# Hybrid decoder layer on one core: the sums of weight blocks spread otherwise over the weight loads

## The chip, the cores and the metric

The kernel runs on one core of one Trainium2 chip. The metric is the device time of one execution in microseconds (us), smaller is better. The core has a matrix engine (TensorE, PE in the profile, its weight loads PEld), three engines for elementwise work (VectorE: DVE, ScalarE: ACT, GpSimd: POOL), and 16 DMA engines that are fed here by two queues: SP's (the profile's q1) and POOL's (q0).

## The reference

One layer over 512 positions of width 1024, all in float32:

```python
h = rms_norm(x, norm_mix)
hq, hf, hi, hg, mq, mk, mv = split(h @ w_in)          # one projection, 3584 columns
o_hgrn = hgrn2_mixer(hq, hf, hi, hg, lb, hgrn_norm)   # gated linear recurrence, chunks of 32
o_moba = moba_attention(rotary(mq), rotary(mk), mv)   # causal attention over chosen blocks
x = x + concat(o_hgrn, o_moba) @ w_out
h, mem_n = rms_norm(x, norm_xattn), rms_norm(mem, norm_mem)     # mem: 256 tokens
x = x + cross_attention(h, mem_n, w_q, w_k, w_v, w_o)           # 4 heads
h = rms_norm(x, norm_mlp)
x = x + square(relu(h @ w_ff1)) @ w_ff2               # 1024 -> 4096 -> 1024
out = rms_norm(x, norm_final)
```

## The kernel before

**Weight units.** All weights pass through the core as units of 128 rows by 1024 columns (512 KB), in the order in which PE uses them. Units 0 to 3 belong to the columns hf, 4 to 7 to hi, 8 to 11 to hq, 12 to 15 to mv, 16 to 23 to mq and mk (`mkq`), 24 to 27 to hg. From unit 28 (`W_WO`) a list named `line` sets the order: the eight units of the out-projection (`wo`) and the eight of the cross-attention query (`xq`), mixed with units of the memory products (keys and values of the 256 memory tokens; `memX`, `memY` in the profile), and last the eight units `xo` of the cross-attention's output. Unit 80 (`MLP`) begins the first MLP product in 8 groups (`j`) of 7 steps (`s`), unit 136 (`FF2`) the second MLP product.

**What happens to a unit.** SP's queue loads it from DRAM into a raw buffer `wr` (there are three, `RAWS`). Each float32 product is made as three matmuls of a high and a low part: ACT makes the high part `wh` of the weights, DVE the remainder `wl`, and with the end of that DVE instruction the raw buffer is free for a later unit. `need(u)` stands at the start of a unit's matmuls; it issues the splits up to two units ahead (`SPLIT_AHEAD`) and as many loads as there are raw buffers, which makes five units ahead. Instructions of an engine run in the order of the program. In the stretch of units 8 to 12 that order has, besides the splits, the work of the recurrence: DVE makes decayed queries `qx` and keys `ke`, and PE multiplies them (`a`, `ket`).

**The sums.** The memory products and both MLP products are computed with seven block products instead of eight. For that some weight blocks are added to others beforehand, in DRAM, by transfers alone: `copy` (L237) goes on SP's queue, `add` (L240) is an accumulating transfer on POOL's queue, and `values` (L269) are plain transfers on POOL's queue. For the memory weights the sums go to four pairs of blocks, `m0` to `m3` (`MU`), for the second MLP weight to 24 units `u0`, `u1`, `u2` (`FU`). The generator `all_sums()` gives these 88 steps in one fixed order: values into m0 (each step two transfers of 256 KB), adds into m0, four copies into m2, values into m3 (four steps of two transfers), four copies into m1, eight adds into m2 and m1, four adds into m3; then 16 copies into u0 and u2, 16 adds into u0 and u2, 8 copies into u1, 16 adds into u1. `more_sums()` issues the next step, whatever it is, and binds it to `marks[-2]`, the last matmul in front of the previous `need`: so the step's transfers wait until that matmul is done.

Where `more_sums()` is called sets the time of each sum: in `load_unit`, as often as `sums_after(u)` says, right behind the load of unit u; in `need` for the last units ahead of the MLP; and in `f1_prep`, once in a group of the first MLP product. `sums_after` gave two steps with each load of units 8 to 11 and from 16 on, three from 22 on, two with each load of `wo`, one with each of `xo`.

Of the kernel before, what the change touches and what calls it, by code (L numbers as in the profile page):

```python
# [31 lines left out]
W_HG, W_WO, W_MEMK, W_XQ, W_MEMV, W_XO, W_MLP = 24, 28, 36, 44, 52, 60, 68  # L32
MEM_P = 7
MEM_UNITS = 2 * MEM_P * 2
MLP = W_MLP - 16 + MEM_UNITS
# [90 lines left out]
def hybrid_layer(ctx: ExitStack, tc: tile.TileContext, xT, memT, ws, vecs, consts, rots, out):  # L126
# [91 lines left out]
    line, keys = [], iter(KEYS + VALUES)  # L218
# [86 lines left out]
    def more_sums():  # L305
        dma = next(transfers, None)
        for d in dma if isinstance(dma, list) else [dma] if dma is not None else ():
            tc.add_manual_dep(d.ins, marks[-2].ins.name, AFTER)
# [6 lines left out]
    def load_unit():  # L315
        u = state["load"]
        raws[u] = raw_tile(f"wr{u}", u >= FF2 and (u - FF2) % 2 == 1)
        if len(sources[u].shape) == 3:
            SY.dma_start(raws[u].rearrange("p (n c) -> p n c", n=4), sources[u])
        else:  # L320
            SY.dma_start(raws[u], sources[u])
        state["load"] += 1
        for _ in range(sums_after(u)):
            more_sums()

    def sums_after(u):

        if u < W_WO:
            return 2 * (8 <= u < 12 or u >= 16) + (u >= 22)
        if u < MLP:  # L330
            return {"wo": 2, "xo": 1}.get(line[u - W_WO][0], 0)
        return u % 2 == 0 and (4 <= u - FF2 < 14 or u - FF2 >= 26)

    W_MV = 12
# [5 lines left out]
    def split_raw(u, raw, a, b, eng=None):  # L340
        rounded = A.activation(his[u][:, a:b], raw[:, a:b], AF.Copy)
        if u == 6:
            tc.add_manual_dep(rounded.ins, first_root[0].ins.name, BEHIND)
        elif u == W_MV:
            tc.add_manual_dep(rounded.ins, last_decay[0].ins.name, BEHIND)

        def lower(hi=his[u], lo=los[u]):
            (eng or V).tensor_sub(lo[:, a:b], raw[:, a:b], hi[:, a:b].bitcast(F32))
        later(lower)
# [4 lines left out]
    def split_begin():  # L354
        u = state["split"]
        his[u] = wpool.tile([P, D], F32R, tag="whi", name=f"wh{u}", bufs=WBUFS)
        if u < MLP - 4 and u % 4 == 0:
            los[u] = ep.tile([P, D], F32R, tag="wloe", name=f"wl{u}", bufs=1)
        else:
            los[u] = wpool.tile([P, D], F32R, tag="wlo", name=f"wl{u}", bufs=WBUFS - 1)  # L360
        state["split"] += 1
        return u

    def split_unit(eng=None):
        u = split_begin()
        split_part(u, 0, D, eng)
        del raws[u]
# [7 lines left out]
    def f1_load(j, what):  # L375

        r, c = {"A": (0, 0), "B": (0, 0), "C": (1, 1), "D": (1, 0)}[what.upper()]
        t = f1raw[what, j] = raw_tile(f"w{what}{j}", what in "AD")
        nc.sync.dma_start(two(t), E[r][c][j].rearrange("n p c -> p n c"))
        if what in "Bc":  # L380
            nc.gpsimd.dma_start(two(t), E[0][1][j].rearrange("n p c -> p n c"), accum_op=ALU.add)

    def f1_add(j, out, x, y):
        V.tensor_add(f1raw[out, j], f1raw[x, j], f1raw[y, j])

    def f1_prep(j, s):

        split_raw(split_begin(), f1raw[("ABACcDd" if j == 7 else "ABADcCD")[s], j], 0, D)
        if s == 1 and j == 0:
            f1_add(j, "A", "B", "C")  # L390
        if j == 7:
            if s == 1:
                f1_load(j, "d")
                state["load"] = FF2
            elif s > 3:
                load_unit()
        elif s == 1:
            f1_load(j + 1, "B")
        elif s == 2:
            f1_load(j + 1, "A")  # L400
        elif s == 4:
            f1_load(j + 1, "c")
        elif s == 5:
            f1_load(j + 1, "C")
        elif s == 6:
            f1_load(j + 1, "D")
        if s == 2 and j < 7:
            more_sums()

    def need(u, ahead=SPLIT_AHEAD):  # L410
        marks.append(last_mm[0])
        if MLP <= u + SPLIT_AHEAD < FF2:
            f1_prep(*divmod(u + SPLIT_AHEAD - MLP, 7))
            return
        last = MLP if u < MLP else UNITS
        most = RAWS if u < MLP else 2 * RAWS
        want_load, want_split = min(last, u + LOAD_AHEAD + 1), min(last, u + ahead + 1)
        while state["split"] < want_split or state["load"] < want_load:
            if state["load"] < want_load and state["load"] - state["split"] < most:
                load_unit()  # L420
            elif state["split"] < want_split:
                split_unit()
            else:
                break
        if MLP - 6 <= u < MLP - 2:
            for what in ("A", "B", "cC", "D")[u - MLP + 6]:
                f1_load(0, what)
        if MLP - 8 <= u < MLP - 2:
            more_sums()


# [66 lines left out]
    def fm_stage(u0, act, n, evac, name, groups, order=tuple(range(KT)), o=slice(None), bank=acc_bank, between=None):  # L498


        u = 0
        at = u0 if callable(u0) else lambda n: u0 + n
        for size, late in groups:
            accs = []
            early, rest = order[:KT - late], order[KT - late:]
            for j in range(size):
                need(at(u + j))
                accs.append((bank(u + j) if between else bank)(f"{name}{u + j}"))
                for k in early:
                    fm_k(at(u + j), accs[j][:, :n], act, k, k == order[0], k == order[-1], o)  # L510
                if not late:
                    evac(u + j, accs[j])
                    if between:
                        between(u + j)
            if late:
                for j in range(size):
                    for k in rest:
                        fm_k(at(u + j), accs[j][:, :n], act, k, False, k == order[-1], o)
                    evac(u + j, accs[j])
                    if between:  # L520
                        between(u + j)
            u += size

    def tm_stage(u0, act, ntok, evac, name, beside=()):

        accs = [(side_bank if t in beside else acc_bank)(f"{name}{t}") for t in range(ntok)]
        for j in range(4):
            need(u0 + j)
            hi, lo = his[u0 + j], los[u0 + j]
            for t in range(ntok):  # L530
                for kk in range(2):
                    a_hi, a_lo = act(2 * j + kk)
                    a_hi, a_lo = a_hi[:, t * P:(t + 1) * P], a_lo[:, t * P:(t + 1) * P]
                    w_hi, w_lo = hi[:, kk * T:(kk + 1) * T], lo[:, kk * T:(kk + 1) * T]
                    st = j == 0 and kk == 0
                    mm(accs[t], a_hi, w_hi, st, False)
                    mm(accs[t], a_hi, w_lo, False, False)
                    mm(accs[t], a_lo, w_hi, False, j == 3 and kk == 1)
                if j == 3:
                    evac(t, accs[t])  # L540
# [199 lines left out]
    for k in range(KT):  # L740
        if k % 2 == 0:
            need(k // 2, SPLIT_AHEAD - (k == KT - 2))
        if k == KT - 1:
            next(norm_x)
            lower_bounds()
            ordered.__exit__(None, None, None)
        a_hi, a_lo = x_act(k)
        for hs in ((0, 1), (2, 3)) if k in (0, 2) else ((0,), (1,), (2,), (3,)):
            w = {h: [by_k(t[k // 2])[:, h, k % 2] for t in (his, los)] for h in hs}
            for h in hs:  # L750
                mm(accs[h], w[h][0], a_hi, k == 0, False)
            for h in hs:
                mm(accs[h], w[h][1], a_hi, False, False)
            for h in hs:
                mm(accs[h], w[h][0], a_lo, False, k == KT - 1)
        if k == 0:
            cols = [slice(n * P, (n + 1) * P) for n in range(QE)]
            for acc, c in zip(q_accs, cols):
                mm(acc, q_hi[:, c], a_hi, True, False)
            for acc, c in zip(q_accs, cols):  # L760
                mm(acc, q_lo[:, c], a_hi, False, False)
            for acc, c in zip(q_accs, cols):
                mm(acc, q_hi[:, c], a_lo, False, False)
# [3 lines left out]
    u = 4  # L767
# [614 lines left out]
    u = MLP  # L1382
# [437 lines left out]
```

## Time and profile before

| | us |
|---|---|
| median of three runs | 722.6 (721.71 to 723.08) |
| profiled execution | 723.61 |
| its span | 721.8 |
| PE busy | 710.6 |
| DVE busy | 578.9 |
| ACT busy | 452.4 |
| POOL busy | 81.3 |

The span is the time from the first to the last instruction of the profiled execution; the execution's own time is a little longer. PE's granted clock has a mean of 0.994 of full speed. An instruction row of the timeline reads: start, duration, engine, line, operation, output and inputs, and in brackets the idle time of the engine ahead of it and what ended it. A DMA row gives the size and the median time from issue to landing. Names are without buffer numbers, so all unit loads are called `wr<-in_ws_dram`, or `wr<-m` and `wr<-u` where a sum is loaded.

### The profile page before, as it was taken

What the parts mean: (1) busy time and instruction counts of PE and PEld (TensorE: products, weight loads), DVE (VectorE), ACT (ScalarE), POOL (GpSimd) and SP (SyncE); (2) the same over time, 40 slices, a digit from 0 to 9 for tenths busy, and PEclk for the clock granted to TensorE, in tenths of its full rate; (3) what the DMA queues carried; (4) which work ended last, traced back from release to release, by engine and by line L of the source; (5) the groups of instructions that cost most, each with busy time, mean ns of one, the idle gap of its engine ahead of it and who ended that gap; (6) DMA issues with size and microseconds to landing.
All of it is one profiled execution on the core that took longest, in us unless ns stands there. A gap on an engine that the chain in (4) does not pass through costs nothing.

```text
span 721.8 us, 10716 instructions
## 1 busy us (share of the span) xinstructions
PE 710.6 (98%) x4024; PEld 612.4 (85%) x4024; DVE 578.9 (80%) x878; ACT 452.4 (63%) x659; POOL 81.3 (11%) x98
## 2 busy tenths in 40 slices
PE   9999999999999899999999999999999999999995
PEld 7888888888888788888788989999999888888885
DVE  5899547988786677777578789989889999987886
ACT  6883585446685586666565765666558655547672
POOL 1410205100001000002201101111010100110000
PEclk9999999999999999999999999999999999999998
DMA  8795469999478855458996487778987966998523
GB/s 277 254 227 171 171 215 211 275 312 298 177 200 237 253 185 175 161 189 190 279 289 147 130 211 206 210 190 223 231 199 248 294 222 191 277 275 247 187 77 116
DMA packets 62803, 155.71 MB, mean 216 GB/s; under 512 B 5248, under 2 KB 19456, under 8 KB 62240
## 3 DMA queue, kind: packets, MB, share of 16 engines
q1 hardware_dynamic: 47552, 116.70, 46.5%
q0 software_dynamic: 14592, 37.75, 28.3%
q8 instruction: 31, 0.51, 0.3%
q10 hardware_dynamic: 608, 0.59, 0.3%
q14 instruction: 20, 0.16, 0.1%
HBM read 152.92 MB, written 48.23 MB: 279 GB/s over the span
## 4 chain that ended last, share of the span: by engine, by line
PE 95%; DMA 3%; ACT 1%; DVE 1%; issue 0%; DVEq 0%; SPq 0%; ACTq 0%
PE Y L118 16%; PE X L118 12%; PE xo L118 7%; PE XB L118 6%; PE XA L118 6%; PE mkq L118 6%; PE xq L118 6%; PE wo L118 5%; PE mv L118 3%; PE hq L118 3%; PE hf L118 3%; PE hg L118 3%; PE Z L118 3%; PE hi L118 3%; DMA wr<-in_ws_dram 2%; PE memX L118 2%
## 5 line engine op out<-in xcount | busy, mean ns | idle before, releaser
L118 DVE TENSOR_TENSOR wl<-wr,wh 128x1024 fp32r<-128x1024 f32 (+2 forms) x139 | 165.6, 1196 | 39.2 <-ACT wh L118 32.6
L118 ACT ACTIVATE wh<-wr 128x1024 fp32r<-128x1024 f32 (+2 forms) x139 | 142.7, 1036 | 79.0 <-PE X L118 16.3
L118 PE MATMUL X<-op,wh 128*128 128x512 f32 (+1 forms) x264 | 62.9, 385 | 0.0
L240 POOL DMA_DIRECT2D u<-in_ws_dram x32 | 28.1, 923 | 287.9 <-PE xt L118 90.9
L118 PEld LDWEIGHTS X<-op,wh 128*128 128x128 f32 x264 | 47.2, 189 | 8.5
L118 PE MATMUL Y<-op,wh 128*128 128x512 f32 x192 | 47.2, 391 | 0.0
L118 PEld LDWEIGHTS Y<-op,wh 128*128 128x128 f32 x192 | 35.0, 189 | 6.6
L118 PEld LDWEIGHTS X<-op,wl 128*128 128x128 f32 x256 | 33.6, 191 | 1.6
L118 PE MATMUL X<-op,wl 128*128 128x256 f32 x256 | 34.1, 282 | 0.0
L118 PE MATMUL Y<-OS,wh 128*128 128x256 f32 x256 | 33.4, 283 | 0.0
L118 PEld LDWEIGHTS Y<-OS,wh 128*128 128x128 f32 x256 | 32.5, 192 | 0.7
L118 DVE TENSOR_TENSOR op<-g,op 128x1024 fp32r<-128x1024 f32 x24 | 29.2, 1219 | 2.8 <-ACT op L118 2.8
L118 ACT ACTIVATE op<-g 128x1024 fp32r<-128x1024 f32 x28 | 29.2, 1044 | 0.4 <-PE XB L118 0.4
L118 ACT ACT_TABLE_LOAD x20 | 25.7, 1283 | 2.1 <-PEq L1808 1.2
L118 PEld LDWEIGHTS Y<-op,wl 128*128 128x128 f32 x192 | 25.3, 191 | 1.3
L118 PE MATMUL Y<-op,wl 128*128 128x256 f32 x192 | 25.7, 282 | 0.0
L118 PE MATMUL mkq<-xlo,wh 128*128 128x512 f32 x64 | 25.7, 401 | 0.0
L118 PE MATMUL xq<-x1hi,wl 128*128 128x512 f32 x64 | 25.5, 399 | 0.0
L118 PE MATMUL wo<-mixhi,wh 128*128 128x512 f32 x64 | 25.4, 396 | 0.0
L118 PE MATMUL mkq<-xhi,wl 128*128 128x512 f32 x64 | 25.4, 396 | 0.0
L118 PE MATMUL xq<-x1hi,wh 128*128 128x512 f32 x64 | 25.3, 395 | 0.0
L118 PE MATMUL mkq<-xhi,wh 128*128 128x512 f32 x64 | 25.3, 395 | 0.0
(384 smaller groups left out, 1905.9 us busy)
## 6 DMA issues: line engine op xcount, KB each, us to landing
wr<-in_ws_dram SPq DMA_DIRECT2D x87, 512.0 KB, 5.4
u<-in_ws_dram POOLq DMA_DIRECT2D x32, 512.0 KB, 8.5
wr<-u SPq DMA_DIRECT2D x32, 512.0 KB, 5.1
u<-in_ws_dram SPq DMA_DIRECT2D x16, 512.0 KB, 9.0
wr<-m SPq DMA_DIRECT2D x16, 512.0 KB, 4.1
m<-in_ws_dram POOLq DMA_DIRECT2D x12, 512.0 KB, 12.2
m<-in_ws_dram POOLq DMA_DIRECT2D x16, 256.0 KB, 5.3
u<-u SPq DMA_DIRECT2D x8, 512.0 KB, 5.7
```

The lines of the kernel that those rows point to most:

```text
L118: return f(*args, **kw)
L240: return nc.gpsimd.dma_start(dst, src, accum_op=ALU.add, max_dma_last_dim=4 * D)
```

## The change

Three tables of numbers are changed, and no computation. Two steps go with each load of units 12 to 15 too, where none did. From there on each step of the list goes with a load four units earlier, until the loads of `wo`, which get one step each instead of two. So by the last load of `wo` 54 steps have gone out in both kernels, and 62 by the last of `xo`. The extra calls in `need` begin one unit later (five instead of six), and the last group of the first MLP product makes one step as the others do.

```diff
     def sums_after(u):
         if u < W_WO:
-            return 2 * (8 <= u < 12 or u >= 16) + (u >= 22)
+            return 2 * (u >= 8) + (u >= 22)
         if u < MLP:
-            return {"wo": 2, "xo": 1}.get(line[u - W_WO][0], 0)
+            return line[u - W_WO][0] in ("wo", "xo")
...
-        if s == 2 and j < 7:
+        if s == 2:
             more_sums()
...
-        if MLP - 8 <= u < MLP - 2:
+        if MLP - 7 <= u < MLP - 2:
             more_sums()
```

The order of the instructions of PE, DVE and ACT is the same in both kernels; only the queues of SP and POOL change, and on POOL's most rows keep their order and wait for another matmul. SP's queue around the load of unit 12, before (`wr12` is the load of unit 12, `m2_0` the first block of m2):

```order
L118 DMA wr10_476<-in_ws_dram 128x1024
L118 DMA wr11_544<-in_ws_dram 128x1024
L118 DMA wr12_582<-in_ws_dram 128x1024
L118 DMA wr13_646<-in_ws_dram 128x1024
L118 DMA wr14_714<-in_ws_dram 128x1024
L118 DMA wr15_752<-in_ws_dram 128x1024
L237 DMA m2_0_108<-in_ws_dram 128x2x512 x2
L118 DMA wr16_838<-in_ws_dram 128x1024
L237 DMA m2_1_109<-in_ws_dram 128x2x512 x2
L118 DMA wr17_948<-in_ws_dram 128x1024
```

And the same place now:

```order
L118 DMA wr10_476<-in_ws_dram 128x1024
L237 DMA m2_0_108<-in_ws_dram 128x2x512 x2
L118 DMA wr11_544<-in_ws_dram 128x1024
L237 DMA m2_1_109<-in_ws_dram 128x2x512 x2
L118 DMA wr12_582<-in_ws_dram 128x1024
L118 DMA wr13_648<-in_ws_dram 128x1024
L118 DMA wr14_718<-in_ws_dram 128x1024
L118 DMA wr15_760<-in_ws_dram 128x1024
L237 DMA m1_0_106<-m0_0_104 128x2x512 x2
```

All four copies into m2 now stand ahead of unit 12's load, two of them ahead of unit 11's too; the copies into m1 stand behind unit 15's. On POOL's queue the eight transfers into m3 come next, as before, and wait for matmuls ahead of units 8 and 9 in place of units 12 and 13.

DVE's rows behind unit 12's load, which are the same in both kernels (the numbers are of the changed one; `ke3` is a key block of the recurrence, `qx0` decayed queries of head 0):

```order
L118 TENSOR_TENSOR ke3_695<-Fz_247,ss3_675 128x384
L118 TENSOR_TENSOR qx0_703<-hq0_253,eb0_453 128x2x128
L118 TENSOR_TENSOR wl12_757<-wr12_582,wh12_756 128x1024
L118 TENSOR_TENSOR qx0_703<-qx0_703,dc0_490 128x2x64
L118 TENSOR_TENSOR qx0_703<-qx0_703,ee0_486 128x2x32
L118 TENSOR_TENSOR q4_705<-qx0_703,pp0_487 128x256
L118 TENSOR_TENSOR qx1_704<-hq0_253,eb0_453 128x2x128
```

Nothing moved here: the steps of `qx0` stand behind the split of unit 12 in both.

POOL's queue in the first MLP product, as the difference of the two (`wB`, `wc`: accumulating transfers of the groups' own weights, with the group's number; `u1`: the sums of the second MLP weight):

```order
+L381 DMA wc5_4841<-in_ws_dram 128x2x512
+L381 DMA wB6_4945<-in_ws_dram 128x2x512
 L240 DMA u1_0_88<-in_ws_dram 128x1024
-L381 DMA wc5_4842<-in_ws_dram 128x2x512
-L381 DMA wB6_4946<-in_ws_dram 128x2x512
+L381 DMA wc6_5028<-in_ws_dram 128x2x512
+L381 DMA wB7_5131<-in_ws_dram 128x2x512
 L240 DMA u1_1_89<-in_ws_dram 128x1024
```

The first adds into u1 come one group later each.

## The prediction

> **What bounds the kernel now.** I read the page's shares first, then the waits of PE, then the chain in order of time at the one large wait, then the stretch of the program that receives the moved transfers.
>
> ```profile
> span 721.8 us, 10716 instructions
> PE 710.6 (98%) x4024; PEld 612.4 (85%) x4024; DVE 578.9 (80%) x878; ACT 452.4 (63%) x659; POOL 81.3 (11%) x98
> q1 hardware_dynamic: 47552, 116.70, 46.5%
> q0 software_dynamic: 14592, 37.75, 28.3%
> ```
>
> PE is busy all but 11.2 us of the span. The change touches no matmul, so it can only take away or add PE waits. The queues of SP (q1) and POOL (q0) together fill three quarters of the DMA engines: transfers that start earlier collide with others.
>
> The waits of PE (us in total, times, longest):
>
> ```profile
> PE memY L118 <- ACT wh L118: 1.1, 1, 1.1
> PE memY L118 <- DVE wl L118: 0.8, 1, 0.8
> PE xt L118 <- ACT xp L118: 0.5, 1, 0.5
> ```
>
> The list has no other wait behind a weight load. The two memY waits are one place, weight unit 42. The chain in order of time there (start, us, engine):
>
> ```profile
> 232.72 1.07 ACT wh L118
> 233.82 1.24 DVE wl L118
> 235.07 8.35 DMA wr<-in_ws_dram
> 243.53 1.06 ACT wh L118
> 244.61 1.24 DVE wl L118
> 245.90 2.25 PE memY L118 x5
> ```
>
> With three raw buffers, unit 42's load is issued (235.07) when unit 39's split frees one (DVE, 233.82 + 1.24), takes 8.35 us, and PE waits for it. PE's instructions in time, the wait in brackets, and behind them a row of the windows (stretch; busy us of PE, PEld, DVE, ACT, POOL; clock; DMA share; GB/s):
>
> ```profile
> 242.97 0.39 PE L118 MATMUL memY<-wl,mo 128*128 128x512 f32 x1
> 243.19 0.39 PE L118 MATMUL memY<-wh,mo 128*128 128x512 f32 x1
> 244.63 0.49 PE L118 MATMUL memY<-wh,mo 128*128 128x512 f32 x1 [1.05 <-ACT wh L118]
> 245.90 0.54 PE L118 MATMUL memY<-wl,mo 128*128 128x512 f32 x1 [0.77 <-DVE wl L118]
> 249.64 0.39 PE L118 MATMUL wo<-mixlo,wh 128*128 128x512 f32 x1
> ...
> 246.20:249.70 3.50, 3.50 (x10) 2.70 (x9) 3.07 (x5) 2.76 (x4) 0.00 (x0) 0.51 0.64 193
> ```
>
> Spacing is 243.19 − 242.97 = 0.22 at full clock. After the wait the granted clock is 0.51 for 3.5 us. Counted at 0.227 (mean spacing before), the matmul of 249.64 is the eleventh after 243.19 and would start at 245.69: the place costs **3.95 us**, 1.82 of waiting, the rest the slow clock and the gaps it leaves.
>
> Why the loads are late: two accumulating transfers each (POOL, L240), then unit 39's load on SP's queue with its time to landing, and an add by itself for comparison, near 325.5:
>
> ```profile
> 223.48 1.66 POOL L240 DMA_DIRECT2D u<-in_ws_dram  x2 [15.12 <-PE wo L118]
> 233.00 1.66 POOL L240 DMA_DIRECT2D u<-in_ws_dram  x2 [7.86 <-DMA xr<-in_xT_dram]
> 225.34 0.33 SPq L118 DMA_DIRECT2D wr<-in_ws_dram  x1
> wr<-in_ws_dram SPq DMA_DIRECT2D x1, 512.0 KB, 7.3
> u<-in_ws_dram POOLq DMA_DIRECT2D x1, 512.0 KB, 5.3
> ```
>
> Unit 39's load takes 7.3 behind the first pair; unit 42's takes its 8.35 behind the second.
>
> **Part 1: one sum with each load of wo instead of two.** At 223.48 and 233.00 one add stands in place of a pair. One 512 KB add fewer beside unit 39's load: it lands about 2.7 us earlier (half of a single add's 5.3), so unit 42 is issued near 232.4, and by the same 2.7 takes some 5.6 and lands near 238. PE needs the split's first half at 243.42, so the load needs to be in by 242.2: slack some 4 us. Gain 3.95. Bounds: 0 (one add delays as much as two) to −3.95. I take −3.95, since each half of the chain needs to win only 1.2 us of its 2.7.
>
> **Part 2: two sums with each load from unit 12 to 15, and everything behind them four loads earlier.** The DMA engines get the same transfers at other places. The place that matters is behind units 8 to 11. Four copies on SP that followed units 15 and 16 now follow units 10 and 11, ahead of unit 12's load; eight plain transfers of 256 KB on POOL wait for the start of units 8 and 9 on PE instead of 12 and 13. There the engines stand so (windows, columns as above; then DVE and ACT, and PE, in time; then the load of unit 12, its issue and its time):
>
> ```profile
> 44.00:50.00 6.00, 6.00 (x29) 4.95 (x28) 6.00 (x15) 4.45 (x7) 0.00 (x0) 1.00 1.06 231
> 48.00:64.00 16.00, 16.00 (x72) 13.27 (x71) 15.99 (x44) 8.26 (x12) 0.00 (x0) 1.00 0.41 138
> 59.49 1.99 ACT L118 ACTIVATE wh<-wr 128x1024 fp32r<-128x1024 f32 x2
> 62.24 1.21 DVE L118 TENSOR_TENSOR wl<-wr,wh 128x1024 fp32r<-128x1024 f32 x1
> 63.37 0.28 DVE L118 TENSOR_TENSOR qx<-qx,dc 128x128 f32<-128x128 f32 x1
> 64.91 0.21 DVE L118 TENSOR_TENSOR qx<-qx,ee 128x64 f32<-128x64 f32 x1
> 64.49 0.49 PE L118 MATMUL ket<-ident,ke 128*128 128x128 f32 x3
> 64.91 0.32 PE L118 MATMUL a<-qx,kt 128*32 128x32 f32 x5
> 50.16 0.33 SPq L118 DMA_DIRECT2D wr<-in_ws_dram  x1
> wr<-in_ws_dram SPq DMA_DIRECT2D x1, 512.0 KB, 3.2
> ```
>
> DVE has no idle time between 48 and 64 (15.99 of 16.00). Its split of unit 12 (`wl`, 62.24) stands ahead of the `qx` steps that PE's `a` matmuls take at 64.91, with 0.2 us between. So any delay of that `wl` reaches PE. It needs ACT's `wh` of unit 12 first (1.0 us), so the load must land by **61.1**. Now it lands at 50.16 + 3.2 = 53.4, and 7.7 us of slack hide it.
>
> The load's new landing. SP's queue serves in order; unit 10's load lands 7.1 after its issue (first two rows); then seven transfers behind unit 14, first and last, the time of the last, and four of the plain ones where they run now:
>
> ```profile
> 36.97 0.33 SPq L118 DMA_DIRECT2D wr<-in_ws_dram  x1
> wr<-in_ws_dram SPq DMA_DIRECT2D x1, 512.0 KB, 7.1
> 63.48 0.33 SPq L118 DMA_DIRECT2D wr<-in_ws_dram  x1
> 71.95 0.33 SPq L118 DMA_DIRECT2D wr<-in_ws_dram  x1
> wr<-in_ws_dram SPq DMA_DIRECT2D x1, 512.0 KB, 6.1
> m<-in_ws_dram POOLq DMA_DIRECT2D x4, 256.0 KB, 4.4
> ```
>
> From 36.97 + 7.1 = 44.1 on, six transfers of 512 KB go through SP's queue up to unit 12: two copies, unit 11, two copies, unit 12. What one costs lies between two prices. Low: q1's 46.5% of 721.8 us for 116.70 MB is 1.5 us per 512 KB. High: seven such transfers, issued from 63.48 to 71.95, were in at 71.95 + 6.1 = 78.05, so 14.6 us, 2.1 each. I take the middle, 1.8: 10.8 us. Beside them POOL's queue holds the adds that keep the engines full to 50 now (share 1.06); of those 6 us one load (1.5) is SP's, so 4.5 are theirs. Then come the eight plain transfers, released when units 8 and 9 start on PE: at q0's mean price, 28.3% of 721.8 for 37.75 MB, 2.84 us per 512 KB, they would cost 11.4; at SP's low price 6.0, which I take since they are plain reads that ran four at a time in 4.4 us. 44.1 + 10.8 + 4.5 + 6.0 = **65.4**, late by 4.3. Bounds: 44.1 + 6 × 1.5 = 53.1 if POOL's traffic costs SP nothing (in time by 8), and 44.1 + 12.6 + 4.5 + 11.4 = 72.6, which I hold for too far since half of the second four would still be behind unit 12.
>
> So PE waits about 4.3 us at 64.9 (4.1 to 4.5 by the 0.2). The rest of the load is on the clock: the wait of 1.82 at 243 was followed by 3.5 us at 0.51, which is 1.7 lost. I add 1.7. Sum of part 2 here: **+6.0**, between 0 and +9. Should the wait be there, DVE is next late: everything it does up to 74 shifts by the same amount.
>
> Units 8 to 11 themselves: unit 11's load goes behind two copies, and lands, by the same prices, at 44.1 + 3 × 1.8 + 4.5 = 54.0, well ahead of the ACT instructions of 59.49 and of the DVE split that follows its own. I cost it at nothing; if wrong it adds to the same wait, not beside it.
>
> The rest of the shift: the adds into m1, m2, m3 and the copies into u come four loads earlier. The cover is that loads go out five units ahead; the list has no PE wait for a split in these units. If that cover went, one load behind a pair of adds would be late by 8.35 − 3.2 = 5.2 at most, of which a unit's lead takes most. Nothing, 0 to +1.
>
> **Parts 3 and 4: one sum fewer at MLP − 8, one more with group 7 of the first MLP product.** The add at MLP − 8 goes to the next places, one later each, and the u1 adds stand in groups 5, 6, 7 in place of 4, 5, 6. SP and POOL do the same there with one transfer each per group; a load behind an add can be late by 7.3 − 3.2 = 4.1 at most, and the loads of groups 4 to 6 beside such adds give no entry in the list of PE's waits. Nothing; if the cover is gone, up to that 4.1. The wait of 0.5 for `xp` stays.
>
> **Sum.** −3.95 + 4.3 + 1.7 = +2.05. The profiled execution took 723.61 (span 721.8), 1.0 above the median of the three runs shown, 722.6; the sum goes on the median: **724.6**.
>
> **Rivals.** *Unit 12 is in time* (faster): the gain of part 1 stays whole, 722.6 − 3.95 = 718.6. For it: at 48–64 the engines are only 0.41 busy, so 9.4 of 16 us are free, and the low price gives 44.1 + 9.0 + 4.5 + half of the plain ones, 3.0 = 60.6, just within. Against: the middle price. It decides at a landing of 61.1.
>
> *The clock stays full after the wait*: −3.95 + 4.3 = +0.35, 722.95. For it: the wait is one piece, in a stretch of short matmuls. Against: the shorter wait at 243 was followed by 0.51. The Trainium skill ("TensorE: Matmul & The Clock Gate", Part 1: The HAM clock gate) has the half clock come after an idle window of about 3.4 us. By that page's figure the 1.82 us of waiting in two pieces at 243 should have left the clock alone; the measured 0.51 behind it says otherwise, and the measurement decides.
>
> *Part 1 does not remove the stall*, since a pair less at one place only moves the adds of other loads: 722.6 + 6.0 = 728.6. Against: the two pairs shown become two single adds, and the rest lie at earlier loads.
>
> *Nothing shows*: neither term, 722.6.
>
> **How the numbers follow.** The measurement tells 0.2% (1.45 us) from no change: below 721.15 faster, above 724.05 slower. Forecast, unit 12 late by 2 to 7 us with the clock halved: 0.55, times 722.4 to 727.4, of which 0.17 lies under 724.05 (lateness under 3.7). In time: 0.20. Clock full: 0.12, of which 0.03 faster when the wait is under 2.5. Stall stays: 0.06. Nothing: 0.07. Faster 0.20 + 0.03 = 0.23; same 0.17 + 0.09 + 0.07 = 0.33; slower 0.38 + 0.06 = 0.44. The range reaches to the in-time case below and to 727.4 above: 718.3 to 727.4; the forecast's own is 722.4 to 727.4.
>
> **What would show it.** Right: unit 12's load takes over 11 us from its issue; DVE idles several us for ACT's `wh` near 62; PE waits for `qx` near 65 and runs below full clock for some 3 us behind; no memY wait, and full clock, near 243. Wrong: DVE without idle time up to 64, or a load of unit 11 or of 22 to 28 in the list of PE's waits, or a new wait in group 7 of the first MLP product.

## The result, and the profile after

The changed kernel takes 727.67 us (median of six runs, 726.16 to 729.21) against 722.19 for the kernel before (six runs, 721.71 to 723.08): ratio 1.0075, 95% interval 1.0063 to 1.0086. It is **slower by 5.5 us**. The prediction had the sign and the place, 2.0 us in place of 5.5, and a range that ended 0.27 us below the result. One of the eleven executions of the half-copies kernel below took 1436.36 us, has no trace, and is not in that kernel's ratio.

The page after, of the 729.21 us execution, the slowest of the six; first its shares and queues:

```profile
span 727.4 us, 10723 instructions
PE 712.5 (98%) x4024; PEld 614.3 (84%) x4024; DVE 579.1 (80%) x878; ACT 452.4 (62%) x659; POOL 81.0 (11%) x98
q1 hardware_dynamic: 47552, 116.70, 46.3%
q0 software_dynamic: 14592, 37.75, 28.8%
```

The bytes are the same; the work is the same; PE has 14.9 us that are not busy in place of 11.2, and 1.9 more that are busy at a slower clock. The waits of PE (total, times, longest) say where:

```profile
PE a L118 <- DVE qx L118: 6.4, 1, 6.4
PE warm L118 <- POOL eps L601: 1.0, 1, 1.0
PE hf L118 <- ACT xhi L118: 0.2, 1, 0.2
```

The two waits for memY and the one for `xp` are gone; one wait of 6.4 us for `qx` is new. The chain in order of time there:

```profile
50.53 18.81 DMA wr<-in_ws_dram
...
69.44 1.06 ACT wh L118
70.53 1.23 DVE wl L118
71.76 0.35 DVE qx L118 x2
72.15 0.85 PE a L118 x11
```

Unit 12's load is issued at 50.53, almost as before, and takes 18.81 us in place of 3.2. ACT's `wh`, DVE's `wl` and the two `qx` steps follow one upon the other, and PE's `a` goes on at 72.15. The windows of this stretch (stretch; busy of PE, PEld, DVE, ACT, POOL; clock; DMA share; GB/s) show what the wait costs behind it:

```profile
65.70:72.10 6.40, 0.00 (x1) 0.00 (x0) 1.57 (x4) 2.43 (x3) 0.00 (x0) 0.91 0.23 92
72.10:75.60 3.50, 3.44 (x51) 2.53 (x52) 3.50 (x11) 0.06 (x1) 0.00 (x0) 0.50 0.69 239
75.60:79.10 3.50, 3.50 (x15) 3.05 (x15) 2.66 (x9) 1.33 (x2) 0.00 (x0) 0.69 0.99 332
```

Behind the wait the granted clock is 0.50 for 3.5 us and 0.69 for the next 3.5: 1.75 + 1.09 = 2.8 us lost. Where the wo loads are, the stretch in which the stall stood is now full, at full clock:

```profile
235.00:253.00 18.00, 18.00 (x81) 14.88 (x81) 11.19 (x13) 9.55 (x12) 0.82 (x1) 1.00 0.92 246
```

The starts of the stages on PE, from the two timelines, give the balance:

| first matmul of | before | after | gained (+) or lost (−) since the row above |
|---|---|---|---|
| hi | 28.90 | 29.27 | −0.37 (start of the execution) |
| mv | 77.25 | 87.22 | **−9.60** (unit 12) |
| memX | 223.02 | 233.01 | −0.02 |
| xq | 256.94 | 262.93 | **+4.00** (stall near 243) |
| xo | 333.11 | 339.50 | −0.40 |
| first MLP product | 398.55 | 404.23 | +0.71 |
| last stretch of X (second MLP product) | 690.57 | 696.25 | 0.00 |

### The profile page after: what moved, and what is told of

It reads as the page before. It is cut to its first block, busy times and chain, and to the rows that moved or that the text cites. A ratio compares the mean times of both kernels' runs of the same rounds, so it can differ in the third digit from the quotient of the medians.

```text
span 727.4 us, 10723 instructions
## 1 busy us (share of the span) xinstructions
PE 712.5 (98%) x4024; PEld 614.3 (84%) x4024; DVE 579.1 (80%) x878; ACT 452.4 (62%) x659; POOL 81.0 (11%) x98
## 4 chain that ended last, share of the span: by engine, by line
PE 92%; DMA 3%; ACT 2%; DVE 2%; issue 0%; DVEq 0%; SPq 0%; ACTq 0%
PE Y L118 16%; PE X L118 12%; PE xo L118 8%; PE XB L118 6%; PE XA L118 6%; PE xq L118 6%; PE mkq L118 6%; PE wo L118 6%; PE mv L118 3%; PE hg L118 3%; PE Z L118 3%; PE memX L118 3%; PE hf L118 3%; DMA wr<-in_ws_dram 3%; PE memY L118 2%; PE xs L118 2%
## 5 line engine op out<-in xcount | busy, mean ns | idle before, releaser
L118 PE MATMUL xq<-x1lo,wh 128*128 128x512 f32 x64 | 25.2, 394 | 0.0
```

What stands on the lines that cost most here:

```text
L118: return f(*args, **kw)
```

## The experiments

Theory A: unit 12's load is late because of what is put ahead of it in SP's queue and beside it in POOL's, and the gain comes from the single adds at wo. The rivals are in the expectations. The first four kernels ran on one chip (before: 723.64 there), the last three on one chip (before: 723.31), so ratios are compared; 727.7, 718 and the like in the expectations count from 722.2.

### Part 2 alone

```diff
-            return 2 * (8 <= u < 12 or u >= 16) + (u >= 22)
+            return 2 * (u >= 8) + (u >= 22)
```

> Part 2 of the change alone: two steps with each load of units 12 to 15, so every later step comes eight steps earlier and the list ends sooner; the loads of wo keep two steps each, the MLP part is as before. Theory A (the loss is unit 12's load behind the moved transfers, the gain is the thinning at wo and at MLP - 8): PE waits about 6.4 us for qx near 65 and loses about 3.2 more to the clock, the wait for memY near 243 (3.6 to 4 us) stays: 722.2 + 9.6 = 731.8. Rival C (the stall near 243 goes because the adds before it come earlier, whatever stands with wo): the stall is gone here too, about 728.

730.88 us (six runs, 724.44 to 733.39), ratio 1.0087 (1.0057 to 1.0118); the profiled run has a span of 731.6. This kernel does not compute the layer: its list ends eight steps sooner, so the last eight adds into u1, which the kernel before issues from 610 us on, have gone out by 582, ahead of u1's first loads, which are to bring the sums without them. The work of PE, DVE and ACT is the same. Its waits:

```profile
PE a L118 <- DVE qx L118: 6.3, 1, 6.3
PE memY L118 <- ACT wh L118: 1.0, 1, 1.0
...
PE memY L118 <- DVE wl L118: 0.8, 1, 0.8
```

Both waits stand side by side, as theory A has it: the loss belongs to part 2, and earlier adds do not remove the stall while wo's loads keep two steps. It is the trace that decides this, not the time: the ratio makes 728.5 of 722.2, nearer to rival C's 728 than to theory A's 731.8. The profiled span is 9.8 us above that of before, but not by theory A's terms: from hi to mv 9.2 were lost, the stall cost 1.5 less than in the trace of before, since the clock stayed at 1.00 behind it, and 1.8 more went between the starts of the two MLP products, which is not explained. The runs spread over 9 us. The one of 724.44 had a mean granted clock of 0.998, the other five 0.992 to 0.995; what else made it fast is not known, since only the first has a trace.

### The wo part alone

```diff
-            return 2 * (8 <= u < 12 or u >= 16) + (u >= 22)
+            return 2 * (8 <= u < 12 or u >= 16) + (u >= 22) + (16 <= u < 24)
...
-            return {"wo": 2, "xo": 1}.get(line[u - W_WO][0], 0)
+            return line[u - W_WO][0] in ("wo", "xo")
```

> The wo part alone: one step with each load of wo instead of two, and the eight steps taken from there go one each with the loads of units 16 to 23; units 12 to 15 carry none, the MLP part is as before. Theory A: no wait near 65, no wait for memY near 243: 722.2 - 3.6 = 718.6. Rival C (the stall depends on something else than the pairs of adds at wo): the wait for memY stays, 722. Rival D (three and four steps with a load of units 16 to 23 make their loads late as at unit 12): a new PE wait between 110 and 195, 722 or more.

719.59 us (five runs), ratio **0.9943** (0.9929 to 0.9957): faster than both kernels, 718.1 on the 722.2 of before. One row is all that its list of PE's waits holds:

```profile
PE warm L118 <- POOL eps L601: 1.0, 1, 1.0
```

And in the windows the stretch of the stall is full and at full clock:

```profile
246.20:249.70 3.50, 3.50 (x17) 2.88 (x17) 3.16 (x4) 1.94 (x2) 0.00 (x0) 1.00 0.64 188
```

Where before had 10 matmuls in these 3.5 us at 0.51, this one has 17. Three and four steps with a load of units 16 to 23 made no wait. Rivals C and D are out.

### Parts 3 and 4 alone

```diff
-        if s == 2 and j < 7:
+        if s == 2:
...
-        if MLP - 8 <= u < MLP - 2:
+        if MLP - 7 <= u < MLP - 2:
```

> The last two edits alone: no step at MLP - 8, one with the last group of the first MLP product. Theory A: the wait of 0.5 us for xp near 350 goes, since no add stands at 344 beside the load that ACT waits for, and nothing else changes: 722.2 - 0.7 = 721.5. The prediction on record: nothing, 722.2. Rival: a wait in the last group of the first MLP product, up to 4 us, 726.

Ratio 0.9996 (0.9987 to 1.0006): no change that the runs can tell, as the prediction on record had it. Theory A's 0.7 us (0.9990) lies within the interval, but its reason is gone, since the wait for `xp` is still there:

```profile
PE xt L118 <- ACT xp L118: 0.3, 1, 0.3
```

In the changed kernel and in the wo part alone it is absent, and in the values-first kernel below, whose MLP part is that of the changed kernel, it is back with 0.5. So the add at MLP − 8 alone does not make it; what does was not followed further.

### What makes unit 12 late

Three kernels vary what goes ahead of unit 12's load (SP's queue) and beside it (POOL's). First, the plain transfers into m3 ahead of the copies into m2 in the list, so that no copy stands before units 11, 12 or 13:

```diff
+        for h in range(2):
+            yield from values(MU[3], h, 1)
         for h, m in R:
             yield copy(part(MU[2], h, m), by_row(ws[rows(h, m), :, :T]))
-        for h in range(2):
-            yield from values(MU[3], h, 1)
```

> The changed kernel, but in the list of steps the plain transfers into m3 (POOL's queue) come ahead of the copies into m2 (SP's queue), so that SP's queue goes from unit 10's load to 11, 12 and 13 with no copy between, while POOL's eight transfers run about 11 us earlier; as many bytes move in the same stretch. Theory A (unit 12's load is late because four copies stand ahead of it in SP's queue): the load lands before 61, no wait near 65: 727.7 - 9.6 = 718.1. Rival B (it is late because of the load on all DMA engines, POOL's plain transfers above all): it lands at 63 or later, PE waits 2 us or more and the clock follows: 722 to 728.

720.11 us, ratio 0.9953 (0.9939 to 0.9967). No wait near 65. Second, the plain transfers behind the copies into m1, so that POOL's queue is empty beside the four copies:

```diff
         for h, m in R:
             yield copy(part(MU[2], h, m), by_row(ws[rows(h, m), :, :T]))
-        for h in range(2):
-            yield from values(MU[3], h, 1)
         for h, m in R:
             yield copy(part(MU[1], h, m), part(MU[0], h, m))
+        for h in range(2):
+            yield from values(MU[3], h, 1)
```

> The changed kernel with the eight plain transfers into m3 (POOL's queue) put behind the copies into m1, so that POOL's queue is empty from the end of the m0 adds on, while all four copies into m2 stay ahead of unit 12's load in SP's queue. Theory A (queue and shared engines add up): eight transfers at 0.75 us fewer beside it, unit 12 lands near 69.3 - 6 = 63.3, PE waits 0.5 to 1.5 us, half of the loss goes at least: 719 to 721.5. Rival (the copies from DRAM to DRAM are slow by themselves): landing 66 or later, PE waits over 3 us, 723 or more. Rival (only POOL's transfers matter): landing before 58.

719.84 us, ratio 0.9951 (0.9938 to 0.9964), no wait near 65. Third, two copies, the plain transfers, then the other two copies:

```diff
-        for h, m in R:
+        for h, m in R[:2]:
             yield copy(part(MU[2], h, m), by_row(ws[rows(h, m), :, :T]))
         for h in range(2):
             yield from values(MU[3], h, 1)
+        for h, m in R[2:]:
+            yield copy(part(MU[2], h, m), by_row(ws[rows(h, m), :, :T]))
```

> The changed kernel with the list ordered two copies into m2, the eight plain transfers into m3, the other two copies: two copies stand ahead of unit 12's load in place of four, and the eight plain transfers run beside it some 5 us earlier. Theory A: two copies fewer, which took 61.6 - 58.05 and 67.6 - 61.6 = 9.6 us together in the changed kernel: unit 12 lands near 59.8, in time, 718.1 to 719. Rival B (all bytes in the stretch count, in whatever queue order): lands at 66 or later, PE waits 3 us or more, 723 to 727.

721.64 us, ratio 0.9975 (0.9964 to 0.9986). Unit 12's load, time to landing, in the kernel with the values first (issued at 50.71):

```profile
wr<-in_ws_dram SPq DMA_DIRECT2D x1, 512.0 KB, 7.7
```

With the values late (issued at 50.40):

```profile
wr<-in_ws_dram SPq DMA_DIRECT2D x1, 512.0 KB, 10.0
```

And with half the copies (issued at 51.08):

```profile
wr<-in_ws_dram SPq DMA_DIRECT2D x1, 512.0 KB, 10.3
```

The last of these kernels is the only one with a wait of PE here:

```profile
PE a L118 <- DVE qx L118: 1.0, 2, 0.8
```

Its DVE in time shows unit 11's split, which came late:

```profile
60.08 1.23 DVE L118 TENSOR_TENSOR wl<-wr,wh 128x1024 fp32r<-128x1024 f32 x1 [1.96 <-ACT wh L118]
```

| kernel | copies ahead | plain transfers beside | unit 12 lands | PE's wait | hi to mv against before |
|---|---|---|---|---|---|
| before | 0 | 0 | 53.4 | none | |
| values first | 0 | 8 | 58.4 | none | 0.0 |
| values late | 4 | 0 | 60.4 | none | 0.1 |
| half | 2 | 8 | 61.4 | 1.0 | 2.0 |
| changed | 4 | 8 | 69.3 | 6.4 | 9.6 |

Neither the copies nor the plain transfers alone pass the 61.1; together they pass it by 8.2. So the rivals that name one queue alone are out, and "all bytes in the stretch count, in whatever order" is out too: from 40 to 64 us values first moves more than the changed kernel (324 GB/s against 306) with the DMA engines as full, and lands unit 12 in time. The changed kernel, then values first:

```profile
40.00:64.00 24.00, 24.00 (x108) 19.88 (x107) 22.12 (x72) 14.46 (x23) 5.94 (x8) 1.00 1.05 306
40.00:64.00 24.00, 24.00 (x108) 19.87 (x107) 23.73 (x74) 16.76 (x25) 5.96 (x8) 1.00 1.06 324
```

The sizes missed, though: values late was expected near 63.3 with a short wait and came in at 60.4 with none; half copies landed 1.6 later than expected and lost 2.0, not through unit 12 but through unit 11, whose split held DVE idle for 1.96 just ahead.

### The split of unit 12 on POOL

```diff
-            (eng or V).tensor_sub(lo[:, a:b], raw[:, a:b], hi[:, a:b].bitcast(F32))
+            (nc.gpsimd if u == W_MV else eng or V).tensor_sub(lo[:, a:b], raw[:, a:b], hi[:, a:b].bitcast(F32))
```

> The changed kernel with the remainder wl of unit 12 alone computed on POOL in place of DVE, so that DVE's qx steps no longer stand behind it. Unit 12's load is as late as before (two of POOL's plain transfers now go behind it). Theory A1 (DVE's order is what carries the delay, as the prediction had it): no PE wait near 65, 727.7 - 9 = 718.7. Theory A2 (ACT's order carries it as well: wh of units 12 and 13 stand ahead of the copy kets, which the pd matmuls need): PE waits for kets instead, until about 72.4 in place of 72.15 for qx but having done a and four hq matmuls by then, a wait of some 5.2 us, clock as before: 726.5.

724.69 us (12 runs), ratio 1.0016 (1.0002 to 1.0029), against 1.0075 for the changed kernel. PE's wait near 67:

```profile
PE pd L118 <- ACT kets L118: 1.9, 1, 1.9
```

Unit 12's load (issued at 50.62):

```profile
wr<-in_ws_dram SPq DMA_DIRECT2D x1, 512.0 KB, 16.1
```

The windows behind the wait, at half clock:

```profile
72.00:74.00 2.00, 2.00 (x11) 1.27 (x13) 1.93 (x7) 1.06 (x1) 0.00 (x0) 0.50 0.94 348
```

And ACT in time in the changed kernel, where the same order holds:

```profile
69.44 1.06 ACT L118 ACTIVATE wh<-wr 128x1024 fp32r<-128x1024 f32 x1 [7.78 <-DMA wr<-in_ws_dram]
70.72 1.06 ACT L118 ACTIVATE wh<-wr 128x1024 fp32r<-128x1024 f32 x1 [0.22 <-DMA wr<-in_ws_dram]
71.69 0.47 ACT L118 ACTIVATE kets<-ket 128x384 f32<-128x384 f32 x1
```

The wait for `qx` is gone, and a wait for `kets` is in its place: ACT works in order too, and the copy that frees `pd` stands behind the splits of units 12 and 13. That is A2's mechanism; its number, 726.5, was too high and A1's 718.7 too low. Two things are mixed in the time: the order, and a load that lands at 66.7 in place of 69.3, as two of POOL's plain transfers now stand behind the `wl`. PE's order differs a little as well, so the parts were not told apart further.

## Why the prediction was right or wrong

**The stall near 243: right.** −3.95 predicted; the balance gives −4.00, and the wo part alone shows it by itself. Unit 39's load took 5.8 in place of 7.3 and unit 42's 6.4 in place of 8.35, smaller gains than the 2.7 each that I had worked out, but enough:

```profile
wr<-in_ws_dram SPq DMA_DIRECT2D x1, 512.0 KB, 5.8
wr<-in_ws_dram SPq DMA_DIRECT2D x1, 512.0 KB, 6.4
```

The stretch from xq to xo gave 0.40 back.

**The wait at unit 12: right in place, chain and engine; mis-sized in three terms.**

The step that failed is the landing of the load, 65.4 predicted, 69.3 measured. (1) I let the sum start at unit 10's landing of 44.1 as in the trace of before. In the changed kernel the load takes 8.9 in place of 7.1 and lands at 45.9, 1.8 later. The first copies run beside it now, but that they cause this is not shown: it took 7.6 and 8.4 in two other traces without a copy beside it (parts 3 and 4 alone, the wo part alone) and 8.1 in values late with the same copies.

```profile
wr<-in_ws_dram SPq DMA_DIRECT2D x1, 512.0 KB, 8.9
```

(2) The eight plain transfers were taken at 6.0 us, SP's low price. Values late takes them away, and unit 12 lands 8.9 earlier, of which 0.8 is unit 10 (45.1 against 45.9): they cost 8.1. 65.4 + 1.8 + 2.1 = 69.3. The two terms left, 10.8 for SP's six transfers and 4.5 for POOL's adds, make 15.3, and values late has 60.4 − 45.1 = 15.3; that is luck in part, since unit 11 was in 11.4 behind unit 10 there where I had 9.9, and the three transfers behind it took 3.9 where I had 5.4. What goes with a price above the average of SP's queue is seen in the DMA share of the changed kernel:

```profile
60.00:64.00 4.00, 4.00 (x20) 3.30 (x19) 4.00 (x18) 0.81 (x2) 0.00 (x0) 1.00 1.04 379
64.00:66.00 2.00, 1.70 (x16) 1.06 (x14) 0.41 (x2) 0.00 (x0) 0.00 (x0) 1.00 0.87 319
66.00:68.00 2.00, 0.00 (x0) 0.00 (x0) 0.00 (x0) 0.00 (x0) 0.00 (x0) 1.00 0.41 164
68.00:70.00 2.00, 0.00 (x0) 0.00 (x0) 0.00 (x0) 0.56 (x1) 0.00 (x0) 1.00 0.14 55
70.00:72.00 2.00, 0.00 (x0) 0.00 (x0) 1.47 (x3) 1.78 (x3) 0.00 (x0) 0.74 0.07 29
```

Full until 64 and nearly so until 66, then 0.41, 0.14, 0.07 of 16 engines: 6.6, 2.2, 1.1 engines at work on average, while the loads of units 12, 13 and 14 land one after the other at 69.34, 70.62 and 71.88. The trace marks the completion of a load 16 times, which I read as once for each DMA engine's share. Of unit 12's load the first mark came at 59.77, the eighth at 60.71, still ahead of the 61.1, and the last at 69.34; ACT's `wh` began at 69.44. In values late the marks lie between 57.91 and 60.40, in before between 52.93 and 53.40. So half of the load was in on time, and PE waited for the engines that were furthest behind. My prices per transfer were means over the engines and could not show that. Which transfers load those engines more, the trace does not tell.

(3) Late by 8.2, PE waited 6.4. My 0.2 us between DVE and PE was read from the wrong `qx`: the first `a` that must wait needs the steps of 63.37 and 63.57, not that of 64.91, so the slack was about 1.1. The rest is that this execution runs 0.37 later and that PE made eight `a` matmuls (0.42) ahead of its wait. This error went the other way.

```profile
65.28 0.42 PE L118 MATMUL a<-qx,kt 128*32 128x32 f32 x8
72.15 0.37 PE L118 MATMUL a<-qx,Fz 128*32 128x96 f32 x3 [6.45 <-DVE qx L118]
```

**The half clock: right that it follows, too small, and less sure than I took it.** 1.7 taken from the stall of 1.8 us; 2.8 behind the wait of 6.4. By the Trainium skill ("TensorE: Matmul & The Clock Gate", Part 1: The HAM clock gate) an idle window of about 3.4 us brings it. The wait of 6.4 agrees; the 1.9 in the kernel with POOL's split, also followed by 0.50, does not. But a wait of some 2 us does not always bring it. Part 2 alone has the stall of before (1.0 and 0.8), parts 3 and 4 alone a longer one, and in both traces the clock stays at 1.00 behind it. Two windows behind the stall of part 2 alone (PE's waits there end at 253.90 and 255.16), then the waits and two windows of parts 3 and 4 alone:

```profile
253.50:257.00 3.50, 2.35 (x9) 1.53 (x10) 3.12 (x4) 2.66 (x5) 0.00 (x0) 1.00 0.53 159
257.00:260.50 3.50, 3.50 (x17) 2.88 (x17) 2.99 (x4) 2.40 (x3) 0.00 (x0) 1.00 0.79 249
PE memY L118 <- ACT wh L118: 1.8, 1, 1.8
PE memY L118 <- DVE wl L118: 0.8, 1, 0.8
246.20:249.70 3.50, 2.74 (x12) 1.97 (x12) 3.50 (x5) 2.93 (x5) 0.00 (x0) 1.00 0.44 135
250.00:253.50 3.50, 3.50 (x18) 2.88 (x17) 1.93 (x3) 1.37 (x2) 0.00 (x0) 1.00 0.62 211
```

So it was in part chance that the trace of before, from which I took the 1.7, had the half clock at all. What decides it is not shown.

So part 2 came to +9.6 in place of +6.0: 6.4 of waiting and 2.8 of slow clock, and 0.4 that I cannot assign. These 3.6 us are what lies between 2.0 and 5.5; the small rows of the balance cancel out to 0.1.

**Unit 11** I had at 54.0 and without effect. It landed at 58.05 (47.30 + 10.76). Its split was late by 1.6 on DVE, hidden there by the longer wait, and was the whole loss in the half-copies kernel.

**The bounds.** My upper end for the landing was 72.6, and I set it aside because half of the second four plain transfers would be behind unit 12. In the changed kernel all eight landed before unit 12's load, the last at 68.7. The range should have gone to that end.

**Parts 3 and 4: right**, nothing measurable; the wait for `xp` that I said would stay did go (its stretch gained 0.71), without the cause being found. **The rest of part 2: right**: values late makes all other early moves and runs at 0.9951, like the wo part alone at 0.9943.

## What to carry to other kernels

A transfer that nobody waits for still has a price: count what stands ahead of the next needed load in its own queue and what runs beside it in the others, and start that count from the range of landings seen for the first transfer, not from one trace. When a load is late by a sum of terms, each of which alone is within the slack, carry the upper ends into the range, since the sum is what crosses. And look at every in-order engine that stands behind the late load: taking one out of the chain only brings the next one forward.

## What the runs showed of the hardware

With a backlog on both queues the 16 shares of unit 12's load finished 9.6 us apart (59.77 to 69.34, with DMA shares of 0.41, 0.14 and 0.07 behind a full stretch), against 0.5 in before and 2.5 in values late, and ACT could begin only behind the last. PE's clock fell to half behind a single wait of 1.9 us and behind 1.05 and 0.77 in before, and stayed at 1.00 behind 1.0 and 0.8 in part 2 alone, behind 1.8 and 0.8 in parts 3 and 4 alone, and behind 0.8 and 0.2 in the half-copies kernel. So in these traces the length of the wait does not tell by itself whether the clock falls. The half-copies kernel behind its waits:

```profile
66.80:70.30 3.50, 3.14 (x59) 2.37 (x59) 3.50 (x11) 0.34 (x1) 0.00 (x0) 1.00 1.02 329
```
